# The second layer's output weights split a layer ahead and kept in DRAM, with part of two token blocks' output products moved under the last attention head

## The chip, the cores and the metric

The kernel runs on one core of a Trainium2 chip. The metric is the device time of one execution in microseconds (us). A core has five engines with a queue each: PE multiplies matrices, DVE and ACT work on vectors, POOL does general work, SP issues DMAs here. Each engine runs its own queue in the order in which it was written down.

## The reference

A trunk of two layers over x of 1 x 1024 x 1024 in float32, with a token mixer and a SwiGLU block in each, and layer norms after both:

```
for i in range(DEPTH):                       # 2
    mix = _mla_mixer(h, ...) if i % 2 == 0 else _diff_mixer(h, ...)
    h = _layernorm(ALPHA * h + mix, ln_mix_g[i], ln_mix_b[i])
    h = _layernorm(ALPHA * h + _swiglu(h, w_gu[i], w_down[i]), ln_ffn_g[i], ln_ffn_b[i])

def _diff_mixer(...):                        # 8 heads, two softmax maps per head
    logits = einsum('bqhmd,bkhmd->bmhqk', q_b, k) * scale - slopes * dist
    p = softmax(where(chunk_mask, logits, NEG_BIG))
    a = p[:, 0] - lam * p[:, 1]
    o = einsum('bhqk,bkhe->bqhe', a, v)      # v: 128 columns per head
    o = _rmsnorm(o, g_sub) * (1.0 - lambda_init)
    return o.reshape(b, s, 1024) @ w_o       # w_o: 1024 x 1024

def _swiglu(x, w_gu, w_down):
    gate, up = split(x @ w_gu, 2)
    return (silu(gate) * up) @ w_down
```

The mask is causal over chunks of 64 tokens, so a block of 128 rows i sees 128 (i + 1) keys.

## The kernel before

A float32 product is made of three products of a narrower kind (fp32r): an operand is split into a high part (ACT casts it) and a low part (POOL or DVE subtracts the high part from the operand), and `mm3` issues high times high, high times low, low times high, the lines L143, L144 and L145 of the profile. Line L148 is a transpose on PE through an identity.

The stages follow each other on PE: mixer A, its output projection, ffn of layer 0 (500 to 1100 us; the gate and up products to about 855), differential attention (1100 to 1560), its output projection (1558 to 1657), ffn of layer 1. In the ffn the gate and up products come as a stream of units of 12 products; `consume` issues one, `prepare` loads and splits weights some units ahead (gr and gp are the loaded weights, op_g and op_gp their parts; L372 is the cast, L373 the subtract). `op_unit` takes the place of the two parts from rings of tiles named wh and wl; raw loads use a ring wr.

`attention` runs over heads and blocks of 128 rows (the last head in LAST_ORDER = (6, 7, 4, 5, 2, 3, 0, 1)). In a slot it issues the scores of a block two ahead (`s_b`, L216, of bk, the keys, and bq and ql, the queries' two parts), then the turn of the block before (the maximum `mx_b` on DVE, L219; the exponent on ACT; POOL's L1180 and DVE's L1181, which combines the two maps; transposes `pt_b`; split into pth_b and ptl_b) and its products with the values (`o_b`, L255). A table `fill` names other work for a slot, such as the projections of the next heads: `bp` for keys and queries, `bv` for values. These read xT, the layer's input, which is held in stacks that `xst.close()` gives back. The normed heads are written to `o_dr` in DRAM by SP (`norm_b2`, L1220); the last head stays in `ob`.

`out_proj` stands behind the last head in the program. It loads the eight 128 x 1024 pieces of w_o (r_wo), splits each (L136 on ACT, L137 on POOL), and for each block of 128 tokens in LAST_ORDER loads the heads (of), splits them (oh; L315 on ACT, L316 on DVE), loads x (z), multiplies 8 heads x 3 x 2 halves = 48 products of 512 columns (zp_a), adds each half to ALPHA x (L327), and does the layer norm (`layer_norm`: L166 to L183 on DVE, store L184). `raw_x` transposes the block before (xTp_a) for the next ffn. A scheduler sets each engine's order from the dependences, so products of the projection may stand among those of the head before.

Of the kernel before, what the change touches and what calls it, by code (L numbers as in the profile page):

```python
# [9 lines left out]
F32 = mybir.dt.float32  # L10
F32R = mybir.dt.float32r
AF = mybir.ActivationFunctionType
ALU = mybir.AluOpType
# [3 lines left out]
P = 128  # L17
S = 1024
D = 1024
NTB = S // P  # L20
KD = D // P
H = 8
# [7 lines left out]
ALPHA = 4.0 ** 0.25  # L30
# [12 lines left out]
def trunk(  # L43
# [32 lines left out]
    nc = tc.nc  # L76
# [48 lines left out]
    def small(name, n=1):  # L125
        return sp.tile([P, 2], F32, tag="small", name=name, bufs=22)[:, :n]

    def load_w(src, cols, name, hi=None, lo=None, eng=None, raw=None, ins=False):

        if raw is None:  # L130
            raw = wp.tile([P, 1024], F32, tag="wr", bufs=2, name=f"r_{name}")
        nc.sync.dma_start(raw[:, :cols], src)
# [3 lines left out]
        A.copy(hi[:, :cols], raw[:, :cols])  # L136
        j = (eng or G).tensor_tensor(lo[:, :cols], raw[:, :cols], f32(hi[:, :cols]), ALU.subtract)  # L137
        return (hi, j.ins) if ins else (hi, lo)
# [11 lines left out]
    def bcast_row(pool, src, n, name, tag):  # L150
        t = pool.tile([P, n], F32, tag=tag, name=name, bufs=1)
        nc.gpsimd.dma_start(t, src.partition_broadcast(P))
        return t
# [121 lines left out]
                fn()  # L275
        mix(blocks[-1][0], blocks[-1][1] // 2)

    def out_proj(side, w_o, o_dram, x_src, x_dst, lng, lnb, xo, layer, scale=None, last=None):


        with tc.tile_pool(name=f"op{layer}", bufs=2, side=side, reuse_waits="tile") as pool:
            g = bcast_row(pool, lng, D, f"mg{layer}", "g")
            b = bcast_row(pool, lnb, D, f"mb{layer}", "b")
            in_big, in_ring = ((0, 1, 2, 3, 7), (4, 5)) if layer == 0 else ((), (6, 7))
            wo = []
            for h in range(H):
                dst = ()
                if h in in_big:
                    t = big_tile(f"wo{layer}_{h}")
                    dst = (t[:, 0], t[:, 1])  # L290
                elif h not in in_ring:
                    t = pool.tile([P, 2, D], F32R, tag=f"wo{h}", name=f"wo{layer}_{h}", bufs=1)
                    dst = (t[:, 0], t[:, 1])
                wo.append(load_w(w_o[h], 1024, f"wo{layer}_{h}", *dst))

            def pair(name, dt, tag):
                if layer:
                    return big_tile(name, dt)
                return pool.tile([P, 2, D], dt, tag=tag, name=name)

            prev = None
            for tb in LAST_ORDER:
                nm = f"a{layer}_{tb}"
                of = pool.tile([P, H, P], F32, tag="of", name=f"of_{nm}", bufs=2)
                n = H if last is None else H - 1
                src = o_dram[tb // 2][:n, :, (tb % 2) * P:(tb % 2) * P + P]
                nc.sync.dma_start(of[:, :n], src.rearrange("h p q -> p h q"))
                ot = pair(f"oh_{nm}", F32R, "oh").rearrange("p a (h q) -> p a h q", h=H)
                oh, ol = ot[:, 0], ot[:, 1]
                if scale is None:  # L310
                    A.copy(oh, of)
                    V.tensor_tensor(ol, of, f32(oh), ALU.subtract)
                else:
                    for hs, o in ((slice(0, H - 1), of[:, :H - 1]), (H - 1, last(tb))):
                        A.activation(oh[:, hs], o, AF.Copy, scale=scale)  # L315
                        V.scalar_tensor_tensor(ol[:, hs], o, scale, f32(oh[:, hs]), ALU.mult, ALU.subtract)  # L316
                zy = pair(f"zy_{nm}", F32, "zy")
                z, y = zy[:, 0], zy[:, 1]
                nc.sync.dma_start(z, x_src[tb * P:(tb + 1) * P, :])
                sums = small(f"sum_{nm}", 2)  # L320
                junk = []
                for nh in range(2):
                    c = slice(nh * 512, nh * 512 + 512)
                    m = (ps_m if nh == 0 else ps_t)(f"zp_{nm}_{nh}")
                    junk.append(m)
                    mm3(m, [(oh[:, h, :], ol[:, h, :], wo[h][0][:, c], wo[h][1][:, c]) for h in range(H)])
                    V.scalar_tensor_tensor(  # L327
                        z[:, c], z[:, c], ALPHA, m, ALU.mult, ALU.add, accum_out=sums[:, nh:nh + 1]
                    )
                if tb == LAST_ORDER[-1] and not layer:  # L330
                    y = big_tile(f"y_{nm}", F32)[:, 0]
                layer_norm(z, sums, junk, y, g, b, nm, x_dst[tb * P:(tb + 1) * P, :])
                if prev is not None:
                    raw_x(prev[1], xo, prev[0], f"a{layer}_{prev[0]}")
                prev = (tb, y)
        return lambda: raw_x(prev[1], xo, prev[0], f"a{layer}_{prev[0]}")
# [33 lines left out]
    def split(dst, src, eng):  # L370
        hi, lo = dst
        A.copy(hi, src)  # L372
        eng.tensor_tensor(lo, src, f32(hi), ALU.subtract)  # L373
# [12 lines left out]
    def swap(side):  # L386
        return "left" if side == "right" else "right"

    def ffn(side, xo, xst, pending, layer, x_src, x_dst, lng, lnb, next_x):

# [419 lines left out]
        return new, rest, normed  # L810

    o_dr = [[dr.tile([H, P, 256], F32, name=f"o_dr{l}_{g}") for g in range(4)] for l in range(2)]
    xs_dr = [dr.tile([S, D], F32, name=f"xs_dr{l}") for l in range(3)]


# [140 lines left out]
    with ast as st:  # L956
# [97 lines left out]
        def at(slot, fn, *args):  # L1054
            fill.setdefault(slot, []).append(lambda: fn(*args))
# [38 lines left out]
        return new_xT(pool, "f0")  # L1094

    xo, stacks = x_pools("m0", "right")
    pending = out_proj("left", w_o_a, o_dr[0], x, xs_dr[0], ln_mix_g[0], ln_mix_b[0], xo, 0)
    xT, rest, normed = ffn("left", xo, stacks, pending, 0, xs_dr[0], xs_dr[1], ln_ffn_g[0], ln_ffn_b[0], next_x)


    banks("ps3", PS_BUFS_B)
    with ExitStack() as st:
# [91 lines left out]
            return ob[:, h % 2, g * 256:(g + n) * 256]  # L1194

        def last_rows(tb):
            return ob[:, (H - 1) % 2, tb * P:(tb + 1) * P]

        def norm_b(h, g0=0, g1=4):

# [6 lines left out]
        def norm_b2(h, g0=0, g1=4):  # L1207
            parts = []
            for i, (sq, o) in enumerate(sqs.pop((h, g0))):
                m = ps_s(f"ms{h}_{g0}_{i}")[:, :sq.shape[1]]  # L1210
                T.matmul(m, ones, sq, start=True, stop=True)
                parts.append((sq, o, m))
            for r, _, m in parts:
                A.activation(r, m, AF.Ln, bias=eps_rms, scale=1.0)
            for r, o, _ in parts:
                A.activation(r, r, AF.Exp, scale=-0.5)
                G.tensor_tensor(o, o, r, ALU.mult)
            if h < H - 1:
                for g in range(g0, g1):
                    nc.sync.dma_start(o_dr[1][g][h], o_rows(h, g))  # L1220

# [39 lines left out]
        at(8 * H - 5, norm_b2, H - 1, 3, 4)  # L1261
        at(8 * H - 4, norm_b, H - 1, 2, 3)
        at(8 * H - 3, norm_b2, H - 1, 2, 3)
        attention(score_b, turn_b, mix_b, fill, 2, (0, 60))
        norm_b(H - 1, 0, 2)
        norm_b2(H - 1, 0, 2)

    xst.close()
    xo, stacks = x_pools("m1", "left")
    pending = out_proj("right", w_o_b, o_dr[1], xs_dr[1], xs_dr[2], ln_mix_g[1], ln_mix_b[1], xo, 1, gs, last_rows)  # L1270
# [91 lines left out]
```

## Time and profile before

| | us |
|---|---|
| median of 3 runs | 2315.3 (2312.91 to 2316.4) |
| the profiled execution, its own time | 2315.07 |
| its span in the trace | 2313.3 |
| PE busy | 2256.7 |
| DVE, ACT, POOL busy | 1554.6, 1016.2, 890.3 |
| mean granted clock of PE | 0.991 |

The span is what the trace covers; the execution's own time lies 1.8 us above. In the rows that follow an entry of a timeline has the start, the duration, the engine, the line, the operation, the tiles written and read, their shapes and, in brackets, the idle time before it with what ended it. A group has busy time and mean ns of one, then idle time before its instructions. A window has its length, the busy time of each engine with the number of records, the granted clock of PE as a share of full speed, the busy share of the DMA engines and GB/s.

### The profile page before, as it was taken

To read this page: it belongs to the slowest core of one execution; us is meant where nothing else is said; L and a number is where in the kernel's file an instruction comes from. 1 tells how busy PE (TensorE), PEld (TensorE's weight loads), DVE (VectorE), ACT (ScalarE), POOL (GpSimd) and SP (SyncE) were. 2 spreads that over 40 slices of the span, in tenths; PEclk is the share of its full clock that TensorE was granted. 3 is DMA by queue.
4 is the path that set the end of the run, shared out by engine and by line. 5 is a ranking of instruction groups with operands and counts; after the bars stand their busy time and mean duration, and the time that the engine had idled before them with its cause. 6 is when DMAs were issued, how large, how long until landed. Compare 5 with 4: busy or idle time off the path is not lost. (4 is left out here: it accounts for less than half of the span.)

```text
span 2313.3 us, 31077 instructions
## 1 busy us (share of the span) xinstructions
PE 2256.7 (98%) x11410; PEld 1923.6 (83%) x11410; DVE 1554.6 (67%) x2871; ACT 1016.2 (44%) x2088; POOL 890.3 (38%) x696
## 2 busy tenths in 40 slices
PE   8999999999999999999999999979999999999997
PEld 8999997888888887888888898968878888887886
DVE  5677664596666658777476766675586656658777
ACT  4455573342333324454465655563442333324353
POOL 2232241024444435555332433260014444436564
PEclk9999999999999999999999999989999999999999
DMA  5010125444323337453311212143344232337353
GB/s 199 13 34 31 41 72 182 144 143 143 105 98 107 106 125 306 173 206 131 91 42 33 69 35 58 37 144 112 118 149 152 91 113 93 118 132 300 142 203 120
DMA packets 100201, 272.55 MB, mean 118 GB/s; under 512 B 7488, under 2 KB 31168, under 8 KB 90320
## 3 DMA queue, kind: packets, MB, share of 16 engines
q1 hardware_dynamic: 95632, 260.14, 32.0%
q0 software_dynamic: 4416, 10.42, 1.6%
q8 instruction: 90, 1.47, 0.3%
q14 instruction: 63, 0.52, 0.1%
HBM read 197.13 MB, written 69.21 MB: 115 GB/s over the span
## 5 line engine op out<-in xcount | busy, mean ns | idle before, releaser
L372 ACT CAST op_g<-gr 128x512 fp32r<-128x512 f32 x240 | 147.5, 622 | 410.5 <-PE gb L417 229.7
L373 POOL TENSOR_TENSOR op_g<-gr,op_g 128x512 fp32r<-128x512 f32 x104 | 145.6, 1406 | 303.8 <-DVE tmp L508 153.6
L373 DVE TENSOR_TENSOR op_h<-rh,op_h 128x512 fp32r<-128x512 f32 x154 | 164.6, 1100 | 67.2 <-ACT op_h L372 67.1
L417 PE MATMUL ga<-xh_m,op_g 128*128 128x512 f32 x512 | 168.1, 389 | 0.0
L372 ACT CAST op_h<-rh 128x512 fp32r<-128x512 f32 x154 | 92.7, 619 | 147.4 <-PE dx L685 38.4
L685 PE MATMUL dw<-op_w_t,op_h 128*128 128x512 f32 x660 | 151.3, 390 | 0.0
L685 PEld LDWEIGHTS dw<-op_w_t,op_h 128*128 128x128 f32 x660 | 123.6, 188 | 25.9 <-DVE op_h L373 0.4
L373 POOL TENSOR_TENSOR op_w_t<-tt,op_w_t 128x512 fp32r<-128x512 f32 x66 | 99.2, 1507 | 80.0 <-ACT op_w_t L372 75.0
L222 ACT ACTIVATE l_b<-l_b,mx_b 128x256 f32<-128x256 f32 (+7 forms) x128 | 99.5, 778 | 69.0 <-DVE mx_b L219 67.0
L685 PE MATMUL dx<-op_w_b,op_h 128*128 128x512 f32 x528 | 122.6, 392 | 6.2 <-ACT op_w_b L372 3.9
L685 PEld LDWEIGHTS dx<-op_w_b,op_h 128*128 128x128 f32 x528 | 98.4, 188 | 30.0 <-ACT op_w_b L372 4.7
L1180 POOL TENSOR_SCALAR l_b<-l_b,r_b,cst 128x128 f32<-128x128 f32 (+3 forms) x64 | 52.7, 823 | 178.9 <-DVE r_b L224 172.9
L417 PE MATMUL gb<-t4h_f,op_g 128*128 128x512 f32 x352 | 115.9, 390 | 3.0 <-DVE tmp L500 3.0
L417 PE MATMUL gc<-b22h_f,op_g 128*128 128x512 f32 x352 | 115.7, 390 | 2.6 <-ACT op_g L372 2.6
L373 DVE TENSOR_TENSOR op_g<-gr,op_g 128x512 fp32r<-128x512 f32 x136 | 109.9, 809 | 9.8 <-ACT op_g L372 9.6
L417 PE MATMUL gc<-t1h_f,op_g 128*128 128x512 f32 x352 | 115.6, 389 | 0.0
L417 PE MATMUL gb<-t3h_f,op_g 128*128 128x512 f32 x352 | 115.2, 389 | 0.0
L417 PE MATMUL gb<-t2h_f,op_g 128*128 128x512 f32 x352 | 114.9, 389 | 0.0
L417 PEld LDWEIGHTS ga<-xh_m,op_g 128*128 128x128 f32 x512 | 96.1, 188 | 19.8
L373 POOL TENSOR_TENSOR op_g<-s,op_g 128x512 fp32r<-128x512 f32 x40 | 55.4, 1384 | 145.9 <-ACT op_g L372 145.9
L143 PE MATMUL bp<-xT_f,h_wb 128*128 128x512 f32 x256 | 102.9, 402 | 0.0
L145 PE MATMUL bp<-xT_f,l_wb 128*128 128x512 f32 x256 | 101.7, 397 | 0.0
(352 smaller groups left out, 6829.1 us busy)
## 6 DMA issues: line engine op xcount, KB each, us to landing
gr<-in_w_gu SPq DMA_DIRECT2D x44, 1024.0 KB, 6.9
rh<-h_dr SPq DMA_DIRECT2D x28, 1024.0 KB, 5.2
h_dr<-sh SPq DMA_DIRECT2D x22, 1024.0 KB, 5.0
h_dr<-hp SPq DMA_DIRECT2D x22, 768.0 KB, 4.1
tt<-in_w_dn SPq DMA_DIRECT2D x22, 512.0 KB, 7.8
rh<-h_dr SPq DMA_DIRECT2D x14, 768.0 KB, 4.5
z<-xs_dr SPq DMA_DIRECT2D x16, 512.0 KB, 10.2
rw_b<-in_w_dn SPq DMA_DIRECT2D x8, 1024.0 KB, 8.7
```

What stands on the lines that cost most here:

```text
L143: T.matmul(ps_out, lh, rh, start=(i == 0), stop=False)
L145: T.matmul(ps_out, ll, rh, start=False, stop=(i == n - 1))
L222: A.activation(l[:, :n], l[:, :n], AF.Exp, bias=mx, scale=-1.0, accum_out=sm)
L372: A.copy(hi, src)
L373: eng.tensor_tensor(lo, src, f32(hi), ALU.subtract)
L417: T.matmul(o, w[:, a, kc], x[b][:, k, :], start=(first and k == 0 and (a, b) == (0, 0)), stop=(k == 3 and a == 1), skip_group_check=True,)
L685: T.matmul(o, h[:, a, c], w[:, b_], start=(first and (a, b_) == (0, 0)), stop=(last and a == 1), skip_group_check=True,)
L1180: G.tensor_scalar(l1[:, :n], l1[:, :n], r1, nlam, ALU.mult, ALU.mult)
```

## The change

1. `split_wo` is called at 16 places of the first ffn's stream, at every fifth unit from the 40th. Each call loads a half of one head's w_o (128 x 512), splits it with ACT and DVE and stores both parts in `wo_dr`, a new array in DRAM.
2. The second layer's projection becomes the class `OutProj`. It loads the parts from `wo_dr` (six heads whole, two in halves in the rings wh and wl); the casts and subtracts on r_wo are gone.
3. It is opened in a slot of the last head. `early` multiplies six heads of block 6 in three slots and of block 7 in a fourth and adds the results to z; `late` splits and multiplies heads 6 and 7, which now both stay in `ob`. 36 + 36 + 12 of the 384 products then stand under the last head. There are four more adds (L402), no stores to `o_dr` for head 6, and of holds six heads.
4. `rest` does the other six blocks. Their oh and the z of two blocks at a time come from `big_tile`, a ring of five of which two are held, and of from the ring wr or from tiles of z.

The diff, cut to its core:

```
+    class OutProj:
+        HEADS = H - 2
+        def __init__(self, side, w_dr, o_dram, o_here, x_src, x_dst, scale):
...
+            for tb in LAST_ORDER[:2]:
+                self.of(tb)
+            for h in range(H):
+                if h < self.HEADS:
+                    t = self.pool.tile([P, 2, D], F32, tag=f"wo{h}", name=f"wo1_{h}", bufs=1)
+                    nc.sync.dma_start(t, w_dr[h])
...
+        def split(self, tb, hs, o):
+            oh, ol = (t[:, hs] for t in self.oh[tb])
+            A.activation(oh, o, AF.Copy, scale=self.scale)
+            V.scalar_tensor_tensor(ol, o, self.scale, f32(oh), ALU.mult, ALU.subtract)
...
+        def early(self, tb, heads):
+            for nh in range(2):
+                self.product(tb, nh, heads, heads[-1] == self.HEADS - 1)
+            if heads[-1] == self.HEADS - 1:
+                for nh in range(2):
+                    self.added(tb, nh, ALPHA, False)
...
+        def late(self, tb):
+            self.split(tb, slice(self.HEADS, H), self.o_here(tb))
+            first = tb in LAST_ORDER[:2]
+            for nh in range(2):
+                self.product(tb, nh, range(self.HEADS if first else 0, H), True)
+                self.added(tb, nh, 1.0 if first else ALPHA, True)
+        def rest(self, lng, lnb, xo):
...
+            for tb in LAST_ORDER:
+                if tb not in LAST_ORDER[:2]:
+                    self.of(tb)
+                if tb != LAST_ORDER[0]:
+                    self.late(tb)
+                ... layer_norm of tb, raw_x of the block before
@@ ffn @@
+            if i % 5 == 0 and 40 <= i < 40 + 5 * len(spare):
+                spare[i // 5 - 8]()
@@ body @@
+    def split_wo(h, c):
+        cs = slice(c * 512, c * 512 + 512)
+        raw = wp.tile([P, 1024], F32, tag="wr", name=f"pwo{h}_{c}", bufs=2)[:, :512]
+        nc.sync.dma_start(raw, w_o_b[h][:, cs])
+        nc.sync.dma_start(wo_dr[h][:, :, cs], f32(op_unit(raw, V, f"pwo{h}_{c}")))
...
-            if h < H - 1:
+            if h < H - 2:
                 for g in range(g0, g1):
                     nc.sync.dma_start(o_dr[1][g][h], o_rows(h, g))
...
+        b = 8 * (H - 1) - 2
+        at(b, begin_out)
+        for slot, what, args in (
+            (3, "early", (first, (0, 1))), (4, "early", (first, (2, 3))), (5, "early", (first, (4, 5))),
+            (8, "early", (second, tuple(range(H - 2)))), (9, "late", (first,)),
+        ):
+            at(b + slot, lambda what, *a: getattr(proj[0], what)(*a), what, *args)
```

How the engines' orders move, at three places. First PE in the last head. Before, behind the transposes of block 7 (pt_b_7) come scores of the next blocks and products with the values (o_b):

```order
L148 MATMUL pt_b_7_0_15035<-ident,l_b_7_0_14822 128x128 x4
L148 MATMUL pt_b_7_1_15044<-ident,l_b_7_0_14822 128x128 x4
L216 MATMUL s_b_7_1_1_15024<-bk_10082,bq_10080 128x512
L216 MATMUL s_b_7_1_1_15024<-bk_10082,ql_10085 128x512
L255 MATMUL o_b_3_15053<-pth_b_6_0_14983,bvh_0_13825 128x256
L216 MATMUL s_b_4_0_0_15080<-bk_10082,bq_10080 128x320
L216 MATMUL s_b_4_0_0_15080<-bk_10082,ql_10085 128x320
```

After, in the same stretch (zp_a_6_0_0 and zp_a_6_1_0 are the two halves of block 6's projection, wo_1 and wo_2 the weights of heads 1 and 2):

```order
L216 MATMUL s_b_7_1_1_15169<-bk_10186,bq_10184 128x512
L216 MATMUL s_b_7_1_1_15169<-bk_10186,ql_10189 128x512
L394 MATMUL zp_a_6_0_0_15334<-wo_1_15130,oh_a_6_15113 128x512 x2
L394 MATMUL zp_a_6_0_0_15334<-wo_1_15130,ol_a_6_15114 128x512
L394 MATMUL zp_a_6_1_0_15341<-wo_1_15130,oh_a_6_15113 128x512 x2
L394 MATMUL zp_a_6_1_0_15341<-wo_1_15130,ol_a_6_15114 128x512
L216 MATMUL s_b_4_0_0_15225<-bk_10186,bq_10184 128x320
L216 MATMUL s_b_4_0_0_15225<-bk_10186,ql_10189 128x320
L148 MATMUL pt_b_6_0_15256<-ident,l_b_6_0_15050 128x128 x4
L148 MATMUL pt_b_6_1_15269<-ident,l_b_6_0_15050 128x128 x3
L216 MATMUL s_b_4_0_1_15230<-bk_10186,bq_10184 128x320
```

Groups of six products now stand between the last head's scores. Second, DVE at the end of the last head. Before, the combination of the last row block (L1181 into l_b_1_0) follows its reciprocals directly:

```order
L224 RECIPROCAL r_b_1_0_15377<-sm_b_1_0_15375 128x1
L219 ISA l_b_1_1_15379,mx_b_1_1_0_15383<-s_b_1_1_0_15380,bb 128x256
L219 ISA mx_b_1_1_0_15383 128x1
L244 TENSOR_TENSOR ptl_b_2_1_15364<-pt_b_3_0_15391,pth_b_2_1_15363 128x2x128
L224 RECIPROCAL r_b_1_1_15387<-sm_b_1_1_15385 128x1
L1181 SCALAR_TENSOR_TENSOR l_b_1_0_15369<-l_b_1_0_15369,r_b_1_0_15377,l_b_1_1_15379 128x256
```

After (the line is L1298 now):

```order
L383 SCALAR_TENSOR_TENSOR oh_a_4_15769<-of_a_4_15767,cst,oh_a_4_15769 128x768
L383 SCALAR_TENSOR_TENSOR oh_a_5_15860<-of_a_5_15858,cst,oh_a_5_15860 128x768
L244 TENSOR_TENSOR ptl_b_2_1_15545<-pt_b_3_0_15572,pth_b_2_1_15544 128x2x128
L224 RECIPROCAL r_b_1_0_15558<-sm_b_1_0_15556 128x1
L219 ISA l_b_1_1_15560,mx_b_1_1_0_15564<-s_b_1_1_0_15561,bb 128x256
L219 ISA mx_b_1_1_0_15564 128x1
L244 TENSOR_TENSOR ptl_b_0_0_15603<-pt_b_0_0_15600,pth_b_0_0_15602 128x128
L224 RECIPROCAL r_b_1_1_15568<-sm_b_1_1_15566 128x1
L402 SCALAR_TENSOR_TENSOR z_a_6_15115,sum_a_6_15117<-z_a_6_15115,zp_a_6_0_6_15653 128x512
L1307 COPY bo<-o_b_1_15586 128x256
L402 SCALAR_TENSOR_TENSOR z_a_6_15115,sum_a_6_15117<-z_a_6_15115,zp_a_6_1_6_15661 128x512
L1298 SCALAR_TENSOR_TENSOR l_b_1_0_15550<-l_b_1_0_15550,r_b_1_0_15558,l_b_1_1_15560 128x256
```

The splits of blocks 4 and 5 and two adds of block 6 now stand ahead of that combination. Third, DVE among the other blocks. Before, the split of block 2 (oh_a_2) stands ahead of both adds of block 5:

```order
L316 SCALAR_TENSOR_TENSOR oh_a_2_15865<-of_a_2_15863,cst,oh_a_2_15865 128x896
L316 SCALAR_TENSOR_TENSOR oh_a_2_15865<-bo,cst,oh_a_2_15865 128x128
L178 TENSOR_SCALAR ve_a_4_15750<-ssq_a_4_15746 128x1
L183 SCALAR_TENSOR_TENSOR zy_a_4_15688<-zy_a_4_15688,rs_a_4_15752,mb_15471 128x1024
L327 SCALAR_TENSOR_TENSOR zy_a_5_15779,sum_a_5_15781<-zy_a_5_15779,zp_a_5_0_15782 128x512
L327 SCALAR_TENSOR_TENSOR zy_a_5_15779,sum_a_5_15781<-zy_a_5_15779,zp_a_5_1_15808 128x512
```

After:

```order
L402 SCALAR_TENSOR_TENSOR z_a_4_15770,sum_a_5_15862<-z_a_4_15770,zp_a_5_1_15893 128x512
L166 TENSOR_SCALAR nmu_a_5_15919<-sum_a_5_15862 128x1
L167 TENSOR_SCALAR nmu_a_5_15919<-sum_a_5_15862 128x1
L383 SCALAR_TENSOR_TENSOR oh_a_2_15950<-of_a_2_15948,cst,oh_a_2_15950 128x768
L383 SCALAR_TENSOR_TENSOR oh_a_2_15950<-bo,cst,oh_a_2_15950 128x256
```

That split now stands directly behind the last add of block 5 (a tile named z_a_4 holds z of blocks 4 and 5).

More of the change, by code (lines that the diff above doesn't have):

```diff
@@ L276, in attention, with out_proj @@
         mix(blocks[-1][0], blocks[-1][1] // 2)
[L278 to L284, printed above, removed]
+    def out_proj(side, w_o, o_dram, x_src, x_dst, lng, lnb, xo):
+        with tc.tile_pool(name="op0", bufs=2, side=side, reuse_waits="tile") as pool:
+            g = bcast_row(pool, lng, D, "mg0", "g")
+            b = bcast_row(pool, lnb, D, "mb0", "b")
             wo = []
@@ L287, in out_proj @@
                 dst = ()
-                if h in in_big:
-                    t = big_tile(f"wo{layer}_{h}")
+                if h in (0, 1, 2, 3, 7):
+                    t = big_tile(f"wo0_{h}")
                     dst = (t[:, 0], t[:, 1])
-                elif h not in in_ring:
-                    t = pool.tile([P, 2, D], F32R, tag=f"wo{h}", name=f"wo{layer}_{h}", bufs=1)
+                elif h == 6:
+                    t = pool.tile([P, 2, D], F32R, tag=f"wo{h}", name=f"wo0_{h}", bufs=1)
                     dst = (t[:, 0], t[:, 1])
[L294 to L299, printed above, removed]
+                wo.append(load_w(w_o[h], 1024, f"wo0_{h}", *dst))
             prev = None
             for tb in LAST_ORDER:
-                nm = f"a{layer}_{tb}"
+                nm = f"a0_{tb}"
                 of = pool.tile([P, H, P], F32, tag="of", name=f"of_{nm}", bufs=2)
[L305 to L308, printed above, removed]
+                src = o_dram[tb // 2][:, :, (tb % 2) * P:(tb % 2) * P + P]
+                nc.sync.dma_start(of, src.rearrange("h p q -> p h q"))
+                ot = pool.tile([P, 2, D], F32R, tag="oh", name=f"oh_{nm}").rearrange("p a (h q) -> p a h q", h=H)
                 oh, ol = ot[:, 0], ot[:, 1]
[L310 to L317, printed above, removed]
+                A.copy(oh, of)
+                V.tensor_tensor(ol, of, f32(oh), ALU.subtract)
+                zy = pool.tile([P, 2, D], F32, tag="zy", name=f"zy_{nm}")
                 z, y = zy[:, 0], zy[:, 1]
@@ L329, in out_proj @@
                     )
-                if tb == LAST_ORDER[-1] and not layer:
+                if tb == LAST_ORDER[-1]:
                     y = big_tile(f"y_{nm}", F32)[:, 0]
@@ L1096, in trunk @@
     xo, stacks = x_pools("m0", "right")
-    pending = out_proj("left", w_o_a, o_dr[0], x, xs_dr[0], ln_mix_g[0], ln_mix_b[0], xo, 0)
-    xT, rest, normed = ffn("left", xo, stacks, pending, 0, xs_dr[0], xs_dr[1], ln_ffn_g[0], ln_ffn_b[0], next_x)
+    pending = out_proj("left", w_o_a, o_dr[0], x, xs_dr[0], ln_mix_g[0], ln_mix_b[0], xo)
+    def split_wo(h, c):
[3 more added lines that the diff above has]
+        nc.sync.dma_start(wo_dr[h][:, :, cs], f32(op_unit(raw, V, f"pwo{h}_{c}")))
+    xT, rest, normed = ffn(
+        "left", xo, stacks, pending, 0, xs_dr[0], xs_dr[1], ln_ffn_g[0], ln_ffn_b[0], next_x,
+        [lambda h=h, c=c: split_wo(h, c) for h in range(H) for c in range(2)],
+    )
     banks("ps3", PS_BUFS_B)
@@ L1263, in trunk, with begin_out @@
         at(8 * H - 3, norm_b2, H - 1, 2, 3)
+        first, second = LAST_ORDER[:2]
+        proj = []
+        def begin_out():
+            xst.close()
+            proj.append(OutProj("right", wo_dr, o_dr[1], last_rows, xs_dr[1], xs_dr[2], gs))
+        b = 8 * (H - 1) - 2
[5 more added lines that the diff above has]
+            at(b + slot, lambda what, *a: getattr(proj[0], what)(*a), what, *args)
         attention(score_b, turn_b, mix_b, fill, 2, (0, 60))
```

81 lines of the change are left out of this document (75 added, 6 removed).

## The prediction, made before the changed kernel ran

> **What bounds the kernel now.** I read the page first, then a table by windows around the last head, then PE's waits and the timelines of PE, DVE and POOL there.
>
> The page, its busy times and its slices:
>
> ```profile
> span 2313.3 us, 31077 instructions
> PE 2256.7 (98%) x11410; PEld 1923.6 (83%) x11410; DVE 1554.6 (67%) x2871; ACT 1016.2 (44%) x2088; POOL 890.3 (38%) x696
> PE   8999999999999999999999999979999999999997
> PEclk9999999999999999999999999989999999999999
> ```
>
> PE sets the time: it is idle for 56.6 us of 2313.3. The 27th slice (about 1504 to 1562 us) is the only one inside the span that falls to 7, and there the clock falls too. That is the last head of the second layer's attention. By windows (window, length, PE, PEld, DVE, ACT, POOL busy, clock, DMA share, GB/s):
>
> ```profile
> 1510.00:1520.00 10.00, 7.27 (x47) 5.68 (x46) 8.38 (x23) 7.99 (x15) 8.63 (x6) 1.00 0.61 211
> 1520.00:1530.00 10.00, 6.09 (x30) 5.17 (x29) 7.49 (x15) 6.08 (x12) 7.04 (x5) 0.74 0.41 113
> 1530.00:1540.00 10.00, 6.96 (x33) 6.41 (x33) 7.29 (x18) 5.56 (x13) 6.90 (x4) 0.67 0.33 108
> 1540.00:1550.00 10.00, 8.27 (x41) 5.92 (x41) 8.55 (x23) 8.62 (x18) 8.01 (x6) 0.91 0.44 149
> 1550.00:1560.00 10.00, 7.81 (x47) 5.97 (x46) 6.91 (x24) 7.85 (x24) 3.94 (x5) 0.95 0.63 214
> 1562.00:1658.00 96.00, 96.00 (x460) 80.01 (x459) 49.62 (x101) 32.69 (x70) 8.37 (x12) 1.00 0.29 99
> ```
>
> From 1510 to 1560 PE works 36.40 of 50, so 13.6 us are idle; busy time times the missing clock (6.09×0.26 + 6.96×0.33 + 8.27×0.09 + 7.81×0.05) is 5.0 more. 18.6 us are lost in all. DVE is busy 38.62 of the 50: not the bound, but near one. The output projection behind it has PE full for 96 us. What PE waits for in the last head (sum, times, longest), and its longest single wait:
>
> ```profile
> PE pt_b L148 <- DVE l_b L1181: 4.1, 3, 2.4
> PE s_b L216 <- DVE mx_b L219: 3.9, 4, 2.8
> PE s_b L216 <- DVE bk L1166: 2.0, 1, 2.0
> 1526.29 0.64 PE L216 MATMUL s_b<-bk,bq 128*128 128x320 f32 x1 [2.81 <-DVE mx_b L219]
> ```
>
> These are the links of a softmax chain with one head left: scores, maximum, exponent, combination, transpose. Other work on PE would fill them.
>
> **The change: early products (the gain).** 84 products of 512 columns, of 384 in the projection, move from the full stretch behind 1562 into the last head. Their price, at full clock and at half:
>
> ```profile
> 1571.03 0.39 PE L144 MATMUL zp_a<-wo,oh_a 128*128 128x512 f32 x1
> 1571.26 0.39 PE L145 MATMUL zp_a<-wo,oh_a 128*128 128x512 f32 x1
> 1561.24 0.63 PE L144 MATMUL zp_a<-wo,oh_a 128*128 128x512 f32 x1
> 1561.66 0.63 PE L145 MATMUL zp_a<-wo,oh_a 128*128 128x512 f32 x1
> ```
>
> They start 0.23 us apart (0.42 at half clock), so 84 × 0.228 = 19.1 us leave the full stretch. They can save no more than what the last head loses now, 18.6 us, less the waits that stay. These I see in the new order: the first scores still wait 2.0 us for bk; the transposes of the last row block (pt_b_1_0) stand on PE in front of the rest of block 7's products, and on DVE their operand now stands behind two adds into z (0.69 each), a copy and both 768-wide splits of blocks 4 and 5 (about 1.0 each), while PE has only some 14 short products to cover them: 2.8 us, between 0 and 3.4. The fill between them: 36 products go in as six groups of six (1.4 us each), 36 as a run among score products, 12 near the end, so gaps like the 2.8 us one are covered and I expect full clock. Remaining losses 2.0 + 2.8 = 4.8, so the term is 18.6 − 4.8 = **+14**.
>
> [...]
>
> **DVE, POOL and ACT in the last head.** Before, the weights of the projection are split there, eight on POOL, and DVE's combination instruction suffers:
>
> ```profile
> L137 POOL TENSOR_TENSOR wo<-r_wo,wo 128x1024 fp32r<-128x1024 f32 x6 | 14.9, 2492 | 4.3 <-ACT wo L136 4.3
> 1522.27 2.35 POOL L137 TENSOR_TENSOR wo<-r_wo,wo 128x1024 fp32r<-128x1024 f32 x1
> 1522.34 3.23 DVE L1181 SCALAR_TENSOR_TENSOR l_b<-l_b,r_b,l_b 128x896 f32<-128x896 f32 x1 [0.18 <-POOL l_b L1180]
> 1517.72 1.28 DVE L1181 SCALAR_TENSOR_TENSOR l_b<-l_b,r_b,l_b 128x1024 f32<-128x1024 f32 x1
> 1533.16 2.97 DVE L1181 SCALAR_TENSOR_TENSOR l_b<-l_b,r_b,l_b 128x1024 f32<-128x1024 f32 x1
> 1541.22 2.87 DVE L1181 SCALAR_TENSOR_TENSOR l_b<-l_b,r_b,l_b 128x640 f32<-128x640 f32 x1
> L316 DVE SCALAR_TENSOR_TENSOR oh_a<-of_a,cst,oh_a 128x896 fp32r<-128x896 f32 x8 | 9.2, 1148 | 1.6 <-ACT oh_a L315 1.5
> L327 DVE SCALAR_TENSOR_TENSOR zy_a<-zy_a,zp_a 128x512 f32<-128x512 f32 x16 | 11.0, 686 | 33.5 <-PE zp_a L145 33.4
> ```
>
> 1024 columns take 1.28 us free, but 896 take 3.23 when POOL's subtract began 0.07 us earlier. Against 1.15, 1.28 and about 0.85 (640 columns by the 1.28 row) the three blocked ones lose 2.1 + 1.7 + 2.0 = 5.8 us. With POOL's eight subtracts and ACT's eight casts gone, DVE gets that back. It gains four adds of 0.69 (2.8), four 768-wide splits (0.98 by the 896 row; two of them replace 896-wide ones) and two of 256: about 7.5 more. 38.6 − 5.8 + 7.5 = 40.3 us of DVE stand against a stage that becomes 36.4 − 5.0 + 19.1 = 50.5 us of PE: DVE stays under PE, by 10 us. I cost it at nothing beyond the 2.8 above; if cover fails it is the third rival.
>
> **SP and its loads.** Eight loads of 0.5 MB become six of 1 MB and four of 0.5 (8.4 MB), beside block loads; o stores for head 6 go. The six cannot start before the last reader of xT, whose space they take:
>
> ```profile
> 1509.02 0.39 PE L145 MATMUL bp<-xT_f,l_wb 128*128 128x512 f32 x1
> 1513.48 21.92 SPq L132 DMA_DIRECT2D r_wo<-in_w_o_b  x6
> 885.00:890.00 5.00, 5.00 (x24) 4.14 (x23) 5.00 (x4) 0.96 (x2) 4.50 (x3) 1.00 1.04 410
> ```
>
> Loads that queue back to back moved 410 GB/s. From 1509 two z of 0.5 MB and the six stand in line, 7.3 MB: 2.6 us each MB at that rate, so with some 2 us of start the first lands near 1516 and the sixth near 1529. In the new order I add up PE's rows behind that last reader at 0.23 us for 512 columns, less for fewer, with no waits (an estimate): the first group begins 7.6 us behind 1509, at 1516.6, the sixth 24.5 behind, at 1533.5, and the 2.0 for bk push all back. Margins of 2 to 6 us: hidden, at nothing; the second rival is what if not.
>
> **The splits in the first layer's ffn.** 16 loads of 256 KB, 16 ACT casts, 16 DVE subtracts, 16 stores of 512 KB between gate and up products, over some 200 us. The windows 600 to 840 and their groups:
>
> ```profile
> sum 240.00, PE 240.00 PEld 198.77 DVE 148.32 ACT 74.36 POOL 107.27; mean PE 48.00 PEld 39.75 DVE 29.66 ACT 14.87 POOL 21.45
> L373 DVE TENSOR_TENSOR op_g<-gr,op_g 128x512 fp32r<-128x512 f32 x38 | 31.9, 839 | 3.7 <-ACT op_g L372 3.6
> L372 ACT CAST op_g<-gr 128x512 fp32r<-128x512 f32 x76 | 46.7, 622 | 137.9 <-PE gb L417 74.4 <-PE gc L417 25.6 <-PE ga L417 19.7
> ```
>
> 16 × 0.84 = 13.4 us fit in DVE's 92 idle us, 16 × 0.62 = 9.9 in ACT's 166; PE is full and its operands are made ahead. SP's queue carries 32 more transfers; an SP store that waits for its subtract holds the next weight load by about 1 us, with rings in front. Bounds 0 and 16 × (0.62 + 0.84) = 23; I take **−0.5**, near the idle share. [...]
>
> **The other six blocks.** Before, a block's split stands on DVE a block ahead. After, with three rotating buffers, it stands behind the last add of the block before (0.69), then two mean steps, then splits of 768 and 256 columns. PE has beside it:
>
> ```profile
> 1609.60 1.03 PE L148 MATMUL xTp_a<-ident,zy_a 128*128 128x128 f32 x8
> L166 DVE TENSOR_SCALAR nmu_a<-sum_a 128x1 f32<-128x1 f32 x8 | 1.7, 211 | 0.2
> ```
>
> DVE needs 0.69 + 2 × 0.21 + 0.98 + 0.4 = 2.5 us; PE has 1.0 of transposes and four products that need no low half, 0.9. That leaves 0.6 plus the hand-over between engines, about 0.9 for each of blocks 2, 3, 0, 1: **−3.5**, between 0 (the split's buffer comes early) and −4 × 1.6 with the add uncovered.
>
> **The start of the second ffn.** Its first two weight loads stand on SP behind the last store now, and in front of it after:
>
> ```profile
> 1663.66 0.33 SPq L184 DMA_DIRECT2D xs_dr<-zy_a  x1
> 1664.09 1.13 SPq L426 DMA_DIRECT2D gr<-in_w_gu  x2
> 1671.18 0.69 DVE L448 TENSOR_TENSOR gr<-gr 128x512 f32<-128x512 f32 x1 [3.15 <-DMA gr<-in_w_gu]
> 1687.43 0.50 PE L417 MATMUL gc<-b22h_f,op_g 128*128 128x512 f32 x1 [2.62 <-ACT op_g L372]
> ```
>
> DVE waited 3.15 us, and 16 us later PE 2.62 us for an operand of that chain. Between 0 and +3.1: I take **+2.5**, near the wait that is quoted.
>
> **Sum.** 14 − 0.5 − 3.5 + 2.5 = 12.5 off the profiled execution's 2315.07 gives 2302.6; the median of the runs is 0.2 higher, so 2302.8.
>
> **Rivals.**
> - PE gets full through the last head, the clock stays, blocks wait for nothing: 18.6 + 3.1 = 21.7 saved, 2293.6. For it: more movable PE work (19.1) than loss. Against: the in-order waits named above.
> - Loads late (slower). PE runs in order, so each early group holds the whole softmax chain behind it when its weight is not there. The last head's windows show only 108 to 214 GB/s, though with a queue that was never full. Below about 330 GB/s (24.5 us, 2 of start taken off, for 7.3 MB) lateness begins; the 12.5 are eaten when the sixth lands 12.5 later, at 39 us behind 1509, 7.3 MB in 37: 197 GB/s. At 150 it is 49 + 2, 24 late: 2302.8 + 24 = 2327. Against: 410 where a queue was full.
> - DVE or just-in-time splits eat it (same). If the added DVE work lengthens the softmax chain by its full 7.5 us, and blocks cost 6.4: 14 − 7.5 − 6.4 + 2.5 − 0.5 = 2.1 saved, 2313.
> - The first ffn pays (slower): operands late by 1.46 at each of 16 places, 23 lost, 2326. Against: 240.00 of 240 busy with rings ahead.
> - That the change doesn't do what it says is excluded by the order, which shows the products between scores.
>
> **How the numbers follow.** Chances: forecast 0.60, PE full 0.18, splits eat it 0.12, loads late 0.07 (half of it past the point), ffn pays 0.03. 0.2% is 4.6 us, about what runs of this kernel (2312.91 to 2316.4) can tell from no change. Faster (under 2310.7): 0.60 + 0.18 + 0.04 of loads late but short of the point, 0.82; same: the third rival, 0.11 after rounding; slower: 0.03 + 0.04, 0.07. The range goes from the full-PE case with its tails (2315.3 − 21.7 is 2293.6; the half-clock products past 1560 and the runs' own 2.4 below their median aren't counted in it, so 2291) to near the third case (2312).
>
> **What would show it.** Right: the last head's windows at 9.0 or more of 10 busy at full clock, 84 products of L394 in them, the projection's remaining stretch 77 us plus about 3.5 of idle with waits on L383, gr no longer awaited at L448. Wrong: PE waits on wo loads before L394, on L383 for long, or a gap in the first ffn beside L417.

## The result, and the profile after

The changed kernel took 2299.9 us (median of four runs, 2297.0 to 2302.2) where the kernel before took 2315.3: the ratio is 0.994, interval 0.9927 to 0.9952. Two later sets of runs of the same kernel gave 0.9936 (0.992 to 0.9952; 2298.0 against 2313.2) and 0.9924 (0.9911 to 0.9936; 2298.3 against 2315.3). 15 to 17 us were gained; 12.5 were forecast, and 2302.8.

The page after, its first lines and the granted clock by slices:

```profile
span 2300.2 us, 31168 instructions
PE 2253.4 (98%) x11410; PEld 1919.6 (83%) x11410; DVE 1551.7 (67%) x2891; ACT 1017.8 (44%) x2096; POOL 863.9 (38%) x688
PE   8999999999999999999999999999999999999997
PEclk9999999999999999999999999999999999999999
```

PE does the same number of instructions; the 7 and the 8 in the middle of its two rows are gone. The same windows as before (length, PE, PEld, DVE, ACT, POOL, clock, DMA share, GB/s):

```profile
1510.00:1520.00 10.00, 8.22 (x48) 6.65 (x47) 8.60 (x22) 5.84 (x13) 2.33 (x3) 0.88 0.90 338
1520.00:1530.00 10.00, 10.00 (x59) 8.89 (x59) 7.20 (x23) 4.97 (x11) 1.88 (x2) 0.95 1.01 421
1530.00:1540.00 10.00, 10.00 (x64) 9.03 (x63) 8.31 (x27) 6.95 (x18) 1.31 (x2) 1.00 0.58 227
1540.00:1550.00 10.00, 10.00 (x48) 7.75 (x47) 6.36 (x18) 5.68 (x15) 4.23 (x4) 1.00 0.01 2
1550.00:1560.00 10.00, 10.00 (x62) 8.88 (x62) 8.62 (x26) 7.66 (x23) 2.50 (x3) 1.00 0.18 62
1560.00:1570.00 10.00, 7.64 (x40) 6.18 (x40) 8.62 (x23) 5.27 (x16) 4.53 (x5) 1.00 0.58 203
1580.00:1644.00 64.00, 62.76 (x296) 50.37 (x294) 34.65 (x65) 24.54 (x51) 4.70 (x7) 1.00 0.30 107
```

From 1520 to 1560 PE is full. What is left is idle time at the two ends of the last head (1.78 and 2.36 us) and a little clock (8.22 × 0.12 + 10 × 0.05 = 1.5), 5.6 us in all to 1570, where before lost 18.6 to 1560 and some 1.2 of clock behind it (0.88 from 1560 to 1570), under products of the projection. The waits of PE in the last head, and after it to 1700:

```profile
PE pt_b L148 <- DVE l_b L1298: 3.2, 2, 1.9
PE s_b L216 <- DVE bk L1283: 0.5, 1, 0.5
PE zp_a L394 <- ACT zp_a L170: 0.4, 1, 0.4
...
PE gc L520 <- ACT op_g L474: 2.5, 1, 2.5
PE zp_a L394 <- DVE oh_a L383: 0.6, 2, 0.3
PE zp_a L394 <- ACT oh_a L382: 0.6, 3, 0.2
```

To put the gain in its place I measure every trace from the start of the last product that reads xT to the start of the first gate product of the second ffn (the last head and the projection), and from there to the last of that ffn's gate and up products:

| trace | last head and projection, us | gate and up products, us |
|---|---|---|
| before (1509.0, 1657.5, 2083.4) | 148.5 | 425.9 |
| after (1509.7, 1644.1, 2071.0) | 134.4 | 426.9 |
| after, second and third set | 135.4, 135.3 | 424.2, 424.7 |
| products held behind | 144.8 | 427.6 |
| weights split under the last head | 140.1 | 427.0 |
| one block early | 142.8 | 423.5 |
| tail ordered | 134.4 | 426.1 |
| two splits only | 133.9 | 424.3 |
| gate weights on POOL | 134.6 | 430.0 |
| head ordered | 137.1 | 426.8 |
| two splits of the tail on POOL | 139.2 | 424.4 |
| heads 0 and 1 in the rings | 139.5 | 422.0 |
| rings and tail ordered | 137.3 | 422.0 |

13.1 to 14.1 us of the gain lie in that stretch. The other stages differ by 1 to 3 us between traces of one and the same kernel, so the rest of the 15 to 17 is placed only in part: at the start of the second ffn, 0.1 to 1.2 us (below).

### The profile page after: what moved, and what is told of

Its sections match the earlier page's. It is cut to its first block, busy times and chain, and to the rows that moved or that the text cites. A ratio compares the mean times of both kernels' runs of the same rounds, so it can differ in the third digit from the quotient of the medians.

```text
span 2300.2 us, 31168 instructions
## 1 busy us (share of the span) xinstructions
PE 2253.4 (98%) x11410; PEld 1919.6 (83%) x11410; DVE 1551.7 (67%) x2891; ACT 1017.8 (44%) x2096; POOL 863.9 (38%) x688
## 5 line engine op out<-in xcount | busy, mean ns | idle before, releaser
L475 DVE TENSOR_TENSOR op_h<-rh,op_h 128x512 fp32r<-128x512 f32 x154 | 157.8, 1055 | 68.2 <-ACT op_h L474 68.2
L475 DVE TENSOR_TENSOR op_g<-gr,op_g 128x512 fp32r<-128x512 f32 x136 | 111.4, 821 | 17.6 <-ACT op_g L474 17.4
```

## Experiments

Each ran beside the kernel before. Where the changed kernel ran in the same set, medians are compared; where it did not (tail ordered, head ordered, two splits, gate weights on POOL, rings and tail ordered), the ratios to the kernel before are.

**Which half of the change is worth what.** The base of the first set:

> The changed kernel again, as the base for the others on the same chip. Theory F (fill): the 15 us come from 84 products that fill PE's gaps under the last head. Theory W (weights): they come from the eight casts and eight subtracts that left ACT and POOL, and with them DVE's blocked combinations. Both expect 2297 to 2302.

It took 2298.0. First the products are held back:

```
-   at(b + slot, early / late ...)                  # none ahead of block 3's transposes
+   behind(product of blocks 6 and 7, transposes of block 3, last head)
```

> Weights split in the first ffn and kept in DRAM as in the changed kernel, but all products of blocks 6 and 7 held behind the transposes of the last head's block 3, where the first product stands before the change; whole heads 0 to 7 at once. F: the gaps are back, 2307 to 2313, with 10 us or more idle or at half clock between 1510 and 1560. W: the splits are gone all the same, 2298 to 2303.

2309.2 us, ratio 0.9985 (0.9976 to 0.9994): 11.2 of the 15.1 us are gone. Its windows and waits of PE:

```profile
1510.00:1520.00 10.00, 8.22 (x41) 6.42 (x40) 7.86 (x23) 4.44 (x11) 1.68 (x2) 0.83 1.03 421
1520.00:1530.00 10.00, 6.61 (x34) 5.03 (x33) 8.32 (x25) 5.46 (x12) 1.51 (x2) 0.89 1.00 422
1530.00:1540.00 10.00, 9.28 (x53) 7.40 (x53) 7.58 (x25) 7.98 (x21) 2.62 (x3) 0.94 0.21 71
1540.00:1550.00 10.00, 6.64 (x41) 5.56 (x39) 9.21 (x24) 8.22 (x24) 3.94 (x5) 0.91 0.28 104
...
PE pt_b L148 <- DVE l_b L1302: 4.3, 4, 1.9
PE s_b L218 <- DVE mx_b L221: 2.9, 4, 1.4
```

The idle time (9.3 us to 1550) and the low clock are back, with POOL's subtracts still absent. The gaps belong to the softmax chain itself, and the rest of the change without the early products, the relief of ACT and POOL above all, is worth 3.9 us (1.4 to 5.6 by the interval). Held back in this way, 28 products of the projection still stand ahead of the last row block's transposes; before the change 30 did, after it 84. The opposite half, early products with weights split on the spot:

```
-   nc.sync.dma_start(t, w_dr[h])
+   load_w(w_o_b[h], 1024, ..., t[:, 0], t[:, 1])   # ACT cast, POOL subtract
-   the 16 calls of split_wo
```

> Early products as in the changed kernel, but the eight weights loaded and split by ACT and POOL under the last head as before, nothing split in the first ffn. F: most of the gain stays, 2302 to 2307; what goes is DVE's combinations blocked behind POOL's subtracts again (5.8 us by the trace of before) and perhaps waits of the early groups for a weight. W: the gain goes, 2311 to 2315.

2305.4, ratio 0.9964 (0.9949 to 0.9978). PE's waits there, and the window of the tail:

```profile
PE zp_a L389 <- POOL wo L137: 1.3, 2, 1.1
PE zp_a L389 <- ACT wo L136: 0.6, 1, 0.6
...
1560.00:1570.00 10.00, 7.01 (x35) 5.11 (x34) 9.59 (x28) 8.28 (x25) 4.62 (x5) 0.94 0.59 203
```

The early groups wait for a weight being split (1.9 us), and at the end DVE is at 9.59 of 10. Against before: ready weights alone 3.9, early products alone 7.8, both together 15.1. The 3.4 over the sum of the two lies within the intervals of the three numbers; in the table's first column the same shares are 3.7, 8.4 and 13.1 to 14.1, so 1 to 2 us are what the halves do for each other. Then a smaller dose:

```
-   (8, "early", (second, all six heads))           # block 7 behind the last head
```

> Early products for block 6 alone; block 7 is written behind the last head. By the order 66 products instead of 84 stand ahead of the last row block's transposes. F: 18 products of 0.228 us fewer to fill with, 4 us of the gain go where the gaps were filled: 2302 to 2305. W: no difference, 2297 to 2302.

2303.7, ratio 0.9961 (0.9947 to 0.9975): 5.7 us lost where 4 were expected of 18 products. In the table's first column it is 7.4 to 8.4 us. The fill mechanism holds; something else comes with it:

```profile
1550.00:1560.00 10.00, 6.00 (x27) 4.35 (x26) 9.38 (x24) 6.68 (x19) 4.20 (x5) 0.75 0.52 167
...
PE zp_a L395 <- ACT zp_a L170: 2.9, 1, 2.9
```

PE waits 2.9 us in the tail for ACT to be done with a tile of zp_a, into which it writes the layer norm's squares (L170), and the clock is low there.

**The tail of the last head.** The prediction named the wait for the last combination, behind DVE work that the change puts in front of it. In the trace after (PE's row, then DVE's):

```profile
1563.79 0.44 PE L148 MATMUL pt_b<-ident,l_b 128*128 128x128 f32 x2 [1.92 <-DVE l_b L1298]
...
1558.26 1.95 DVE L383 SCALAR_TENSOR_TENSOR oh_a<-of_a,cst,oh_a 128x768 fp32r<-128x768 f32 x2
1561.72 0.67 DVE L402 SCALAR_TENSOR_TENSOR z_a<-z_a,zp_a 128x512 f32<-128x512 f32 x1
1562.65 0.68 DVE L402 SCALAR_TENSOR_TENSOR z_a<-z_a,zp_a 128x512 f32<-128x512 f32 x1
1563.25 0.48 DVE L1298 SCALAR_TENSOR_TENSOR l_b<-l_b,r_b,l_b 128x256 f32<-128x256 f32 x1
```

Splits, adds, then the combination. The first try orders them behind it:

```
+   behind(split of blocks 4 and 5, combination of the last row block)
+   behind(last two adds of block 6, combination of the last row block)
-   (9, "late", (block 6,))                         # written behind the last head instead
```

The third line follows from the second: heads 6 and 7 of block 6 are now written behind the combination. Their products still run ahead of it, and 84 stand ahead of the last transposes as before.

> The changed kernel, with DVE's splits of blocks 4 and 5 (768 columns) and block 6's last two adds ordered behind the combination of the last row block. Theory D: the 1.92 us for which PE waits for that combination come from this DVE work standing in front of it; the wait falls to 0.5 or less and the kernel to about 2296.5 where the changed one has 2298.0 (beside before's 2313.2). Rival: the chain of scores, maximum and exponent sets it; the wait and the time stay.

2298.7, ratio 0.9938 (0.9925 to 0.9952): no gain over the changed kernel's 0.9924 to 0.994. The trace shows why:

```profile
1559.52 0.44 PE L148 MATMUL pt_b<-ident,l_b 128*128 128x128 f32 x2 [0.91 <-DVE l_b L1309]
1562.92 0.38 PE L255 MATMUL o_b<-ptl_b,bvh 128*128 128x256 f32 x1 [1.46 <-DVE ptl_b L244]
...
1560.60 1.94 DVE L391 SCALAR_TENSOR_TENSOR oh_a<-of_a,cst,oh_a 128x768 fp32r<-128x768 f32 x2
1562.46 0.41 DVE L244 TENSOR_TENSOR ptl_b<-pt_b,pth_b 128x256 fp32r<-128x256 f32 x1
```

The first wait halves, and the splits, now later, hold the next operand that PE needs: 0.91 + 1.46 in place of 1.92 + 0.44 (the 0.44 is the wait for ACT's use of a tile of zp_a). Next the work was taken off DVE:

```
+   G.tensor_scalar(of, of, scale, None, ALU.mult); A.copy(oh, of)
+   G.tensor_tensor(ol, of, f32(oh), ALU.subtract)  # blocks 4 and 5, 768 columns
```

> The changed kernel with the 768-wide splits of blocks 4 and 5 done by POOL: the scaling into the raw tile early, the subtract where DVE's stood. Theory D2 (the amount of DVE work at the end of the last head sets the tail, whatever its order): 1.95 us of it gone, so the tail's wait for the last combination falls from 1.92 to 0.5 or less with no new wait for ptl, 1.5 to 2 us faster than the changed kernel. Rival: POOL's subtracts block DVE's two-input operations as before the change, and the wait stays or grows.

2301.3 where the changed kernel has 2298.3 in the same set: slower, with longer waits. PE's waits, and POOL's row:

```profile
PE pt_b L148 <- DVE l_b L1304: 3.9, 3, 2.2
...
1554.64 3.63 POOL L382 TENSOR_TENSOR oh_a<-of_a,oh_a 128x768 fp32r<-128x768 f32 x2 [5.22 <-ACT oh_a L381]
1558.26 0.45 POOL L1303 TENSOR_SCALAR l_b<-l_b,r_b,cst 128x128 f32<-128x128 f32 x1
```

DVE has its 1.95 us free, but its combination needs POOL's own part first, and on POOL that part now stands behind 3.63 us of subtracts. The work ended up in front of the combination on another engine, not in front of a blocked DVE operation, as my rival had it: DVE's rows of 256 columns beside those subtracts (two maxima, a ptl, a copy) took 0.41 to 0.42 us, against 0.42 for a ptl at 1551.59 with POOL idle. So the run doesn't decide whether DVE's amount of work sets the tail: the edit took the work off DVE and put it ahead of the combination's other operand.

**The head of the last head.** PE loses 1.78 us and some clock around 1515. The waits are the same in all three traces of the changed kernel; the clock falls there in the first trace alone. Ordering DVE's split of block 7 behind the combination there:

> The changed kernel with DVE's split of block 7 (768 columns, 1.02 us) ordered behind the combination of head 6's last block. Theory D: the waits of 0.5 us for bk and 1.27 us for that combination at the start of the last head shrink by 1.0 together, and with them the half clock behind them (about 1.5 us of loss): 2295.5 to 2297. Rival: the loads of 0.42 MB per us or POOL's part of the combination set these waits: no change, 2298.

2298.9, ratio 0.994 (0.9927 to 0.9952): no gain. The wait for the combination falls from 1.27 to 0.94, that for bk from 0.50 to 0.39, and PE waits 0.46 us more for ACT (pth_b):

```profile
1511.43 0.68 PE L148 MATMUL pt_b<-ident,l_b 128*128 128x128 f32 x4 [0.94 <-DVE l_b L1307]
```

The waits shrink by 0.4 together and not by 1.0. The clock from 1510 to 1520 is 0.66 here; around the same gaps it was 0.88 in the first trace of the changed kernel and 1.00 in the two others, so it can't be put down to the edit. Then the gap was filled:

```
-   if h < self.HEADS:      # heads 6 and 7 in the rings wh and wl
+   if h >= 2:              # heads 0 and 1 there
```

> The changed kernel a third time, as the base for the two others on the same chip: 2297 to 2302.

> The changed kernel with the parts of heads 0 and 1, in place of 6 and 7, in the rings wh and wl, which are free before xT is: by the order the first three products then stand right behind the values products of head 6, ahead of the scores of block 6. Theory F: they fill the 0.5 and 1.27 us gaps and keep the clock at the start of the last head, where the first trace loses 1.8 us idle and 1.5 us of clock: 2 to 3.3 us faster than the changed kernel. Rival: the ring's tiles come free too late or their loads queue behind others, PE waits for wlo of head 1: same or slower.

2297.4 against 2298.3: the same within the intervals (0.9913 to 0.9938, and 0.9911 to 0.9936). Three rows of PE tell it:

```profile
1516.38 1.06 PE L148 MATMUL pt_b<-ident,l_b 128*128 128x128 f32 x8 [0.45 <-DVE l_b L1298]
1519.25 0.51 PE L394 MATMUL zp_a<-wlo,oh_a 128*128 128x512 f32 x1 [1.22 <-DMA wlo<-wo_dr]
1566.42 0.66 PE L148 MATMUL pt_b<-ident,l_b 128*128 128x128 f32 x2 [4.08 <-DVE nmu_a L166]
```

The early wait falls as expected, a new one of 1.22 comes for a load, and the tail's grows to 4.08 (the row names L166, which ended last; the transposes read the combination, which ran on DVE from 1564.85 to 1566.27 behind two adds). The last kernel joins this with an order of DVE in which the splits of blocks 4 and 5 stand behind the last ptl (heads 6 and 7 of block 6 are written behind the last head again, as in the first try at the tail):

> Heads 0 and 1 in the rings as in the run with the ring first, and DVE's order at the end of the last head set so that what PE waits for comes first: the last combination, then block 6's two adds, the last ptl, and only then the splits of blocks 4 and 5. If the ring's gain at the start (the 1.8 us of waits and the half clock there) was only given back at the tail, where PE waited 4.1 us behind this DVE work, the tail's wait falls to 1 or less and the ratio to the kernel before goes from 0.9926 to 0.9905 to 0.9915 (2292 to 2295 where before has 2313 to 2315). Rival: DVE's amount of work sets the tail in any order, as when only the order was changed: the waits move, the ratio stays at 0.992 to 0.993.

2295.9 against before's 2313.8, ratio 0.9926 (0.9911 to 0.994): the rival's number. It is the lowest median of all, but not to be told from the changed kernel. The waits in its last head:

```profile
PE zp_a L407 <- DMA wlo<-wo_dr: 2.1, 1, 2.1
PE pt_b L148 <- DVE l_b L1313: 1.8, 3, 1.1
PE zp_a L407 <- ACT zp_a L172: 1.2, 1, 1.2
```

The tail's 4.08 became 1.13 for the combination and 1.2 for ACT's use of a tile of zp_a, and the load is waited for longer. But that the time stays is not the rival's mechanism alone. Against the two later traces of the changed kernel, the table has the last head and the projection 2 to 4 us longer with the rings, and the second ffn's gate and up products 2 to 3 us shorter: gr's loads are issued 2.5 us ahead of the first gate product there, instead of 3.3 behind it, and PE's wait for gc's operand is gone (the rows are in the next section).

**The two ffns.** Without 14 of the 16 splits:

> Two of the 16 splits in the first ffn are left in; all heads then load the first head's parts, so the result is not the reference's. Theory D: the splits lie beside a full PE and cost 0 to 0.5: same time as the changed kernel, 2297 to 2299. Rival: they cost what the first ffn's stage was longer in the first trace of the changed kernel, 1.8 us: 2296.

2302.5, ratio 0.9955 (0.9942 to 0.9967): not faster, and outside of what both theories gave. The stage itself, from its first to its last gate or up product, takes 423.3 us here and 421.9 to 424.4 with all 16 splits, so the splits cost nothing that this can show. Why the run is 4 us slower than the tail ordered and the head ordered in its own set stays open; its last head is as short (133.9), and the time is lost before it (3 us more between the first ffn's gate and up products and the last reader of xT) and in the last ffn's end (3 us). For the second ffn, the gate weights' splits moved to POOL:

> The changed kernel with the second layer's gate weights (gp) split by POOL in place of DVE for all six loads. Theory D: at the start of the second ffn DVE is busy without a break from the first gate weight on, and PE's wait of 1.5 to 2.5 us for op_g is set by that amount of work; taking 8 subtracts of 0.68 us off DVE removes the wait: about 2296. Rival: the wait comes from when gr lands; it stays, and POOL's slower subtracts may hold the gates: 2298 or more.

2303.8, ratio 0.9963 (0.9949 to 0.9976), slower, with the wait still there and POOL's subtracts stretched:

```profile
1673.78 1.22 PE L520 MATMUL gc<-t1h_f,op_g 128*128 128x512 f32 x2 [2.56 <-DVE op_g L475]
...
1663.66 1.69 POOL L475 TENSOR_TENSOR op_gp<-gp,op_gp 128x512 fp32r<-128x512 f32 x1 [3.61 <-ACT op_gp L474]
1669.44 8.44 POOL L475 TENSOR_TENSOR op_gp<-gp,op_gp 128x512 fp32r<-128x512 f32 x1 [4.09 <-ACT op_gp L474]
```

It doesn't decide whether DVE's amount of work sets that wait, since POOL and DVE held each other up: the 8.44 us here, and a DVE subtract of 512 columns that took 1.77 beside one of POOL's and 0.68 without.

## Why the prediction was right

- **Early products, +14: right in mechanism and nearly in size.** Last head and projection shortened by 13.1 to 14.1 net of what the blocks gave back (1.2), so 14.3 to 15.3. Holding the products back takes 11.2 us away, so the fill is shown as the main cause. The half clock past 1560 (granted clock before 0.50 from 1560 to 1562, 0.92 to 1564), which the prediction named but left out of its loss, is some 1.2 us of what came beyond 14. Of the residual waits, bk was put at 2.0 and is 0.5 (ACT had two weight casts, 1.99 us, just ahead of bk's cast before, and now has 0.94 us of block 7's split there), the last combination at 2.8 and is 1.92. Not seen were 1.27 us for the first combination and the 1.5 us of clock behind it, which only the first trace has.
- **DVE relieved, costed at nothing: a miss in the bookkeeping.** The ready weights are worth 3.9 us by themselves and 7.3 on top of early products (15.1 less 7.8). I had counted DVE's 5.8 us only against its added work; the term of +14 held it without saying so. The three long combinations of 896, 1024 and 640 columns, 9.07 us together before, took 1.15, 1.27 and 0.88 in the trace after: 5.8 less. DVE's busy time itself came out as added up: 39.1 us from 1510 to 1560, where 40.3 had been forecast.
- **Loads, hidden: right, with luck.** They ran at 421 GB/s; PE's wait for a wo was none here, and 0.2 us in the next two traces.

```profile
1511.20 3.38 SPq L342 DMA_DIRECT2D wo<-wo_dr  x6
wo<-wo_dr SPq DMA_DIRECT2D x6, 1024.0 KB, 16.5
1521.50 0.63 PE L394 MATMUL zp_a<-wo,oh_a 128*128 128x512 f32 x2
```

  The first was forecast to land near 1516 and landed at 1521.2 (10.0 us after its issue), the sixth at 1535.2 instead of 1529: they were issued from 1511.2 on and not from 1509, with two loads of 512 KB from POOL's queue beside them. The 2 us of start were an estimate that the trace of before bears out: r_wo's loads of 512 KB landed a median of 3.6 us behind their issue from 1500 to 1560, 1.3 of it at 410 GB/s. PE reached the first group at 1521.5, also 5 us later than I had added up. The two errors cancel, and the margin was 0.3 us.
- **First ffn, −0.5: right, nearer 0.** The gate and up products run from 450 to 872 us before. PE waits 2.8 us between 499 and 508 in the trace after (0.8 in the trace before), but the first of the new loads is issued at 574.42, so that is not the splits. The stores of the splits held SP's queue for 133.9 us in 16 waits, 8.4 each where about 1 had been put, and from 574 to 872 PE waits 0.4 us in all; in the second trace the stage takes 421.9 us, before 422.6.
- **The other blocks, −3.5: too large.** The five waits on oh between 1606 and 1634 add up to 1.2 us: none for block 2, 0.20 for block 3, 0.49 for blocks 0 and 1 each. There PE does the four products that I counted and then waits 0.29 and 0.34 for the low half. The step that failed is the sum per block: 0.6 of DVE's work uncovered was 0.29 and 0.34 where it came, and two of four blocks have the low half in time. The 0.3 of hand-over no run shows: PE began 0.05 us behind the end of the ACT or DVE row it waited for.
- **Second ffn's start, +2.5: the chain right, the size wrong.** From the first gate product to gc PE takes 29.9 us before, and 29.8, 28.8 and 29.2 in the three traces of the changed kernel, so 0.1 to 1.2 us came. The first trace, and gc in the second:

```profile
1656.50 0.69 DVE L551 TENSOR_TENSOR gr<-gr 128x512 f32<-128x512 f32 x1 [1.17 <-DMA gr<-in_w_gu]
1673.95 0.50 PE L520 MATMUL gc<-b22h_f,op_g 128*128 128x512 f32 x1 [2.50 <-ACT op_g L474]
...
1669.84 0.50 PE L520 MATMUL gc<-b22h_f,op_g 128*128 128x512 f32 x1 [1.48 <-ACT op_g L474]
```

  The step that failed is how much sooner gr lands. Its loads are issued 3.3 us behind the first gate product instead of 6.6, but DVE still waits 1.0 to 1.4 us for them, so its first add on gr comes 1.3 to 2.4 us sooner, where 3.15 had been counted. And from that add to gc it takes 17.4 to 17.5 us, 1.2 more than before (16.2); DVE and ACT work in another order there, and which row costs the 1.2 stays open. That the two waits belong to one chain is shown: the 17.4 to 17.5 us are the same in ten traces, three of the changed kernel and seven of its variants, while the first add comes 10.6 to 13.5 us behind the first gate product. DVE works without a break in between, so what gr is late by, gc is late by. With heads 0 and 1 in the rings and the tail ordered, gr is not awaited and neither is gc's operand:

```profile
1649.71 0.68 DVE L564 TENSOR_TENSOR gr<-gr 128x512 f32<-128x512 f32 x1
1668.75 0.50 PE L533 MATMUL gc<-b22h_f,op_g 128*128 128x512 f32 x1
```

  There the stretch takes 26.9 us, so 3.0 us were to be had, about the upper bound of 3.1.

Of the rivals, the full PE came nearest (2293.6): PE is full from 1520 to 1560 but not at the ends. With 2298.0 and 2298.3 the two later sets lie about midway between that rival and the forecast. That the sum came so close is in part luck: two errors (blocks too dear by 2.3, start too good by 1.3 to 2.4) nearly cancel, and the forecast of 12.5 is short by what the last head gave beyond 14 and by what no stage shows.

## What to carry to other kernels

Where an in-order engine waits inside a latency chain, find independent work of the next stage whose operands can be ready, and make the operands where the engines that prepare them are idle; either half alone gave a quarter to a half of the whole here. Before moving a wait's cause, ask what else that engine owes in the same few microseconds: three reorderings at both ends of the last head only changed which operand was late. An engine that works through its queue without a break passes a wait on in full: here gc came 17.4 to 17.5 us after the first add on gr, however late that was. So ask how much sooner the first operand will land, and not only whether its load stands earlier in its queue.

## What the runs showed of the hardware

The clock fell after short gaps, and not each time. In the trace after, three rows of PE:

```profile
1510.04 0.40 PE L216 MATMUL s_b<-bk,bq 128*128 128x512 f32 x1
1517.35 0.84 PE L148 MATMUL pt_b<-ident,l_b 128*128 128x128 f32 x4 [1.27 <-DVE l_b L1298]
1517.86 0.79 PE L216 MATMUL s_b<-bk,bq 128*128 128x512 f32 x1
```

A product of 512 columns took 0.79 us behind a gap of 1.27 (0.40 at 1510.04), and the window's clock is 0.88; in the second trace of the same kernel the same gap left the clock at 1.00, and it fell to 0.83 (1560 to 1570) behind the later one of 1.92, which left it at 1.00 in the first. The longest single gap in the last head of these two traces is 1.92. What sets off a fall is not shown: each of the two gaps came once with it and once without.

Operations of DVE and POOL took longer beside each other. In the run with the gate weights on POOL, a POOL subtract of 512 columns took 8.44 us (1.69 in the row above it), while DVE ran operations on two operands, 0.68 us each, without a break until 1.2 us before its end. The other way round, in the same trace:

```profile
1655.48 1.67 POOL L475 TENSOR_TENSOR op_gp<-gp,op_gp 128x512 fp32r<-128x512 f32 x1 [3.87 <-ACT op_gp L474]
1655.92 1.77 DVE L475 TENSOR_TENSOR t1l_f<-xr_m,t1h_f 128x512 fp32r<-128x512 f32 x1
1657.62 0.68 DVE L475 TENSOR_TENSOR b22l_f<-xr_m,b22h_f 128x512 fp32r<-128x512 f32 x1
```

The DVE subtract that began 0.44 us behind POOL's took 1.77 us, the next one 0.68.
